# Turning the modulation's rows by 128x128 transposes, with the four groups added on VectorE

## The chip, the cores and the metric

The kernel runs on one core of one Trainium2 chip. The number that counts is the device time of one launch in microseconds (us), as the median of several runs. A profiled execution also leaves a trace, in which each instruction has an engine, a start and a duration.

## The reference, cut to what matters

```python
def first_block(x, c, ctx, c_ctx, w_mod, b_mod, ...):       # two layers, l = 0 and 1
    ...
    for l in range(DEPTH):
        mx = jnp.split((silu_c @ w_mod[l] + b_mod[l])[:, None, :], N_MOD, axis=-1)
        mc = jnp.split(silu_cc @ w_mod[l] + b_mod[l], N_MOD, axis=-1)
        # h = modulate(rms_norm(x), shift, scale): the mixer's input; a gate multiplies its output;
        # the same again for the MLP. mx is for the 256 tokens of x, mc for the 256 of ctx
```

The modulation of a layer is one row vector per condition (c for x, c_ctx for ctx) times a matrix of 1024 x 6144, plus a bias: 6 pieces of 1024, which are the shift, scale and gate of the mixer and of the MLP. The mixer has a Fourier branch, a latent attention branch (keys and values come from a narrow latent `ckv`, queries from `cq`) and a convolution branch, and ends with the product with `w_o`. After the first block comes a second one with another mixer (rwkv, s5 and gla branches), cross attention to a memory `mem`, and a feed-forward part. Everything is fp32.

## The kernel before

Activations lie with features on the 128 partitions and tokens in the free dimension. A large product is made from three products of split values: ScalarE casts a weight to a rounded high half (`wh<-raw`), VectorE subtracts to get the low half (`wl<-raw,wh`), and TensorE adds high x high, high x low and low x high in PSUM. Weights come in chunks of 512 KB (128 x 1024 fp32) through a pool `raw` of four buffers; one queue, SyncE's, issues these loads in the order in which the program asks for them, and a load waits there until its buffer is free.

The modulation of one layer is the generator `modulation(l)`, 24 steps of 256 columns, 48 steps in all. A step takes two loads of `w_mod`. It makes 8 products `md<-raw,cs`, whose stationary operand is the condition (32 columns, two of them used); each runs in one of four groups of 32 rows of the array, so that the group g = k % 4 leaves its partial row of condition i on partition 32g + i of a PSUM half bank. In the trace one such product has two records, so a step has 16. ScalarE copies the half bank to `mrow`. `end` then has to turn the row (columns must come to lie on partitions) and to add the four groups; VectorE adds the bias into `mod`. `end` of a step is called in the next step, so that TensorE has products ahead of it while ScalarE copies. Two half banks alternate.

These steps are fillers. In layer 0's norm, `mixer` calls for one step ahead of each of the eight norm pieces. In the mixer's branches, `weave` goes by a model of the engines' clocks (class `Core`): it takes the first chain whose operands are ready by that model, and prefers the filler where the model says that TensorE would otherwise be too idle. `need_mod` makes the steps that are still missing when a piece of the modulation is used: the first three pieces of layer 0 before `w_o`, the first of layer 1 late in layer 0's MLP. In layer 1's mixer the filler alternates between modulation steps and `memory()`, the keys and values of the second block's cross attention.

So the emitted order depends on the model's cost of every instruction. The model takes `product` for TensorE: an fp32 product costs four passes of the larger of its two widths plus 6 columns, a transpose two passes, and the number of counted columns goes into its notion of how busy TensorE was lately (2 x 2 x 2 for the selecting products of a step, up to 2 x 2 x 128 for two transposes). A scheduler then orders each engine's rows by a modelled time. All recorded instructions have line L243, a helper that passes calls on, so rows are told apart by tiles: `md`, `mrow` and `mod` are the modulation's, `mm` general products, `sc`, `prob` and `pt` attention, `ax` small sums and transposes, `cst_a` the constants (identity, ones and the selecting matrix `sel`).

Of the kernel before, what the change touches and what calls it, by code (L numbers as in the profile page):

```python
# [11 lines left out]
F32 = mybir.dt.float32  # L12
# [4 lines left out]
AX = mybir.AxisListType  # L17
PSUM = bass.MemoryType.PSUM

P = 128  # L20
# [471 lines left out]
class Prog:  # L492
# [241 lines left out]
    def modulation(self, l):  # L734

        nc = self.nc
        mod, ps2 = self.mods[l], self.mdp
        bm = self.v(f"b_mod{l}").rearrange("p (r h f) -> p r h f", r=3, h=2)  # L740
        mv = mod.rearrange("p i (r h f) -> p r h f i", r=3, h=2)

        def end(at, row, ps):
            for h in range(2):
                nc.tensor.matmul(ps[:, 2 * h:2 * h + 2], row[:, h * P:h * P + P], self.c("sel"), start=True, stop=True)
            r, f = at // KD, at % KD
            nc.vector.tensor_add(mv[:, r, :, f, :], ps[:, 0:4].rearrange("p (h i) -> p h i", i=2),
                                 bm[:, r, :, f].unsqueeze(2).to_broadcast([P, 2, 2]))
        last = raw = None

        def half(at, i):
            if l == 0 and self.first:
                return self.first.pop(0)
            return self.raw(self.a[f"w_mod{l}"][at, :, i * 1024:i * 1024 + 1024], 1024)
        for at in range(24):
            self.mark(f"mod{l}")
            raw = [raw or half(at, 0), half(at, 1)]
            ps = ps2[:, at % 2, :]

            for k in range(KD):  # L760
                g = k % 4
                nc.tensor.matmul(ps[32 * g:32 * g + 32, :], self.cs[:, k, :], raw[k // 4][:, k % 4 * T:k % 4 * T + T],
                                 start=k < 4, stop=k >= 4, tile_position=(0, 32 * g))
            row = self.c1.tile([P, T], F32, tag="mrow", bufs=2, name=self.nm("mrow"))
            nc.scalar.copy(row, ps)
            raw = half(at + 1, 0) if at < 23 else None
            if last is not None:
                end(*last)
            last = at, row, ps
            if at % KD == KD - 1:  # L770
                yield [row]
                self.mark(f"mod{l}")
                end(*last)
                last = None
                self.mod_done[l] = at // KD + 1
            yield [raw] if raw is not None else []
# [1736 lines left out]
```

## Time and profile before

| what | value |
|---|---|
| median of 3 runs | 1711.99 us (1711.25 to 1712.37) |
| the profiled execution | 1712.83 us, of which the trace's span is 1711.0 us |
| TensorE busy | 1621.9 us, 95% of the span |
| VectorE, ScalarE, GpSimd busy | 66%, 50%, 5% |
| mean granted TensorE clock | 0.972 of full speed |
| chain of work that ended last | TensorE 84%, VectorE 7%, ScalarE 4%, DMA 3%, issue 2% |
| modulation: the turning products | 192 records, 22.7 to 806.8 us |

The span runs from the first to the last recorded instruction; the execution's own time has 1.83 us more around it. Layer 0's mixer lies at about 25 to 270 us, its MLP up to 670 us, layer 1's mixer at 670 to 830 us, the second block from about 1060 us. A row of the busy table counts an engine's recorded work; a row of the chain says how much of the span is explained by that engine's work when the last instruction is followed back, releaser by releaser.

### The profile page before, as it was taken

The numbers are of one execution on the slowest core, as the hardware profiler recorded it, in microseconds if no ns is written. First come the engines' busy times: TensorE is split into PE (matmuls) and PEld (weight loads), VectorE is DVE, ScalarE is ACT, GpSimd is POOL, SyncE is SP. The second block draws the span as 40 slices with busy tenths as digits, with TensorE's granted clock in tenths as the row PEclk, the third lists the DMA queues.
The fourth block names the chain that finished last, engine by engine and source line by source line (L and its number), as shares of the span: only waits on it lengthen the run. The fifth ranks groups of instructions, "written<-read, shape, count | busy, mean of one in ns | idle before, by whom it ended". The sixth has DMA issues, their size and how long they took to land.

```text
span 1711.0 us, 32233 instructions
## 1 busy us (share of the span) xinstructions
PE 1621.9 (95%) x13240; PEld 1409.6 (82%) x13240; DVE 1123.1 (66%) x2051; ACT 853.2 (50%) x1479; POOL 77.1 (5%) x72
## 2 busy tenths in 40 slices
PE   5999999999999998899999999989989999999997
PEld 2676668888888886766999998878979899999997
DVE  4787536744444457667488866889446769788864
ACT  4436754542323234556565445732357647666643
POOL 0000001000000010000010001001200001010000
PEclk8999999999999999899999999999999999999999
DMA  7724562222322234445545554421113764345543
GB/s 265 238 81 155 189 237 97 84 92 96 99 99 98 87 117 148 172 166 182 180 162 187 184 181 162 147 100 64 40 59 126 253 204 168 124 157 189 177 163 105
DMA packets 69699, 249.61 MB, mean 146 GB/s; under 512 B 7728, under 2 KB 13104, under 8 KB 65712
## 3 DMA queue, kind: packets, MB, share of 16 engines
q1 hardware_dynamic: 69552, 247.55, 42.6%
q8 instruction: 104, 1.70, 0.4%
q14 instruction: 43, 0.35, 0.1%
HBM read 243.33 MB, written 4.19 MB: 145 GB/s over the span
## 4 chain that ended last, share of the span: by engine, by line
PE 84%; DVE 7%; ACT 4%; DMA 3%; issue 2%; SPq 0%; ACTq 0%; DVEq 0%
PE mm L243 65%; PE ax L243 10%; PE md L243 3%; PE sc L243 3%; PE fx L243 2%; DVE y L243 2%; DVE wl L243 2%; DMA raw<-w_mod 1%; ACT L243 1%; ACT wh L243 1%; DVE tmp L243 1%; DVE x L243 1%; DMA x<-xc 0%; ACT y L243 0%; DMA raw<-w_in 0%
## 5 line engine op out<-in xcount | busy, mean ns | idle before, releaser
L243 PE MATMUL mm<-hl,wh 128*128 128x256 f32 (+2 forms) x3856 | 861.3, 319 | 20.5 <-ACT wh L243 7.6
L243 PEld LDWEIGHTS mm<-hl,wh 128*128 128x128 f32 x3856 | 643.5, 193 | 79.8 <-ACT wh L243 9.8
L243 ACT CAST wh<-raw 128x1024 fp32r<-128x1024 f32 (+1 forms) x353 | 361.3, 1025 | 546.0 <-PE mm L243 426.5
L243 PE MATMUL mm<-hl,wl 128*128 128x256 f32 (+1 forms) x1928 | 611.8, 318 | 0.9 <-DVE wl L243 0.8
L243 DVE TENSOR_TENSOR wl<-raw,wh 128x1024 fp32r<-128x1024 f32 (+1 forms) x353 | 421.0, 1194 | 232.5 <-ACT wh L243 231.2
L243 PEld LDWEIGHTS mm<-hl,wl 128*128 128x128 f32 x1928 | 372.0, 193 | 27.2 <-DVE wl L243 3.3
L243 PE MATMUL mm<-y,wh 128*128 128x256 f32 x928 | 169.8, 285 | 7.5 <-DVE early L243 2.6
L243 PEld LDWEIGHTS mm<-y,wh 128*128 128x128 f32 x928 | 144.2, 191 | 9.7 <-DVE y L243 3.1
L243 DVE SCALAR_TENSOR_TENSOR x<-mm,mod,x 128x256 f32<-128x256 f32 x120 | 54.3, 480 | 118.0 <-PE mm L243 117.7
L243 PE MATMUL mm<-y,wl 128*128 128x256 f32 x464 | 131.2, 283 | 0.2 <-DVE wl L243 0.2
L243 POOL TENSOR_TENSOR sq<-sq,sq 128x256 f32<-128x256 f32 (+1 forms) x48 | 58.4, 1217 | 935.9 <-ACT sq L243 787.5
L243 PEld LDWEIGHTS mm<-y,wl 128*128 128x128 f32 x464 | 88.4, 191 | 0.5 <-DVE wl L243 0.4
L243 PE MATMUL mm<-hid,wh 128*128 128x512 f32 x256 | 80.4, 395 | 0.0
L243 PE MATMUL md<-raw,cs 128*32 128x256 f32 x768 | 63.5, 411 | 17.5 <-DMA raw<-w_mod 12.5
L243 DVE SCALAR_TENSOR_TENSOR acc<-u,vec,acc 128x512 f32<-128x512 f32 (+1 forms) x120 | 73.0, 613 | 1.8
L243 ACT ACT_TABLE_LOAD x47 | 60.3, 1283 | 7.9 <-DMA vec<-vec 3.6
L243 PEld LDWEIGHTS md<-raw,cs 128*32 128x32 f32 x768 | 20.1, 112 | 48.2 <-issue 12.2
L243 PEld LDWEIGHTS mm<-hid,wh 128*128 128x128 f32 x256 | 48.0, 187 | 11.7
L243 PE MATMUL mm<-hid,wl 128*128 128x512 f32 x128 | 50.6, 395 | 0.0
L243 DVE TENSOR_REDUCE mx<-sc 128x1 f32<-128x512 f32 (+1 forms) x56 | 31.9, 574 | 20.7 <-PE sc L243 20.3
L243 PE MATMUL sc<-k,hl 96*128 96x512 f32 (+1 forms) x144 | 42.7, 392 | 0.4 <-ACT prob L243 0.2
L243 ACT CAST hl<-tmp 128x256 fp32r<-128x256 f32 (+1 forms) x62 | 28.9, 471 | 27.0 <-DVE tmp L243 27.0
(393 smaller groups left out, 2010.4 us busy)
## 6 DMA issues: line engine op xcount, KB each, us to landing
raw<-w_mlp SPq DMA_DIRECT2D x128, 512.0 KB, 3.3
raw<-w_mod SPq DMA_DIRECT2D x96, 512.0 KB, 4.7
raw<-w_up SPq DMA_DIRECT2D x22, 1024.0 KB, 4.7
raw<-w_gate SPq DMA_DIRECT2D x24, 512.0 KB, 3.3
raw<-w_down SPq DMA_DIRECT2D x16, 704.0 KB, 4.1
raw<-w_in SPq DMA_DIRECT2D x20, 512.0 KB, 4.4
raw<-w_o SPq DMA_DIRECT2D x16, 512.0 KB, 3.9
raw<-w_rw SPq DMA_DIRECT2D x14, 512.0 KB, 3.8
```

Source lines behind the costliest of these rows:

```text
L243: return f(out, *args, **kw)
```

## The change

In `end`, two products of a 128x128 block of `mrow` (stationary) with the 128x2 selecting matrix, which turn the block and add the groups in one go, are replaced with two 128x128 transposes into the same PSUM half bank. The groups then stand side by side as columns 32g + i of each transposed block, and VectorE adds them with one `reduce_sum` over a strided view (4 results of 4 numbers per partition) into a new small tile `mdt` in SBUF with two buffers. The addition of the bias reads `mdt` in place of PSUM.

```diff
@@ -741,11 +741,13 @@
         mv = mod.rearrange("p i (r h f) -> p r h f i", r=3, h=2)
 
         def end(at, row, ps):
+
             for h in range(2):
-                nc.tensor.matmul(ps[:, 2 * h:2 * h + 2], row[:, h * P:h * P + P], self.c("sel"), start=True, stop=True)
+                nc.tensor.transpose(ps[:, h * P:h * P + P], row[:, h * P:h * P + P], self.c("ident"))
             r, f = at // KD, at % KD
-            nc.vector.tensor_add(mv[:, r, :, f, :], ps[:, 0:4].rearrange("p (h i) -> p h i", i=2),
-                                 bm[:, r, :, f].unsqueeze(2).to_broadcast([P, 2, 2]))
+            t = self.sm.tile([P, 2, 2], F32, tag="mdt", bufs=2, name=self.nm("mdt"))
+            nc.vector.reduce_sum(t, ps.rearrange("p (h g q) -> p h q g", h=2, g=4)[:, :, 0:2, :], axis=AX.X)
+            nc.vector.tensor_add(mv[:, r, :, f, :], t, bm[:, r, :, f].unsqueeze(2).to_broadcast([P, 2, 2]))
         last = raw = None
 
         def half(at, i):
```

The program has as many products as before on TensorE (10992 rows in all on that engine), but a transpose has one record in the place of two; VectorE has 48 more instructions (2101 in place of 2053), ScalarE 49 loads of its function tables in place of 47. The model's cost of `end` changes, and so does the order in which `weave` and the scheduler put the work. Steps of the modulation that are issued before layer 0's `w_o` number 40 and a half in place of 33 and a half; the rest follow in layer 1.

The first place is SyncE's queue in layer 0's input products, which issues the loads of weights (`raw_N` is a load's buffer, N only a running number). Before:

```order
L243 DMA raw_467<-w_in 128x1024
L243 DMA raw_473<-w_ukv 128x1024
L243 DMA raw_481<-w_mod 128x1024
L243 DMA raw_493<-w_mod 128x1024
L243 DMA raw_498<-w_in 128x1024
L243 DMA raw_543<-w_in 128x1024
L243 DMA raw_605<-w_in 128x1024
L243 DMA raw_645<-w_in 128x1024
```

And in the changed kernel, from the same load of `w_in` on:

```order
L243 DMA raw_483<-w_in 128x1024
L243 DMA raw_489<-w_ukv 128x1024
L243 DMA raw_497<-w_mod 128x1024
L243 DMA raw_509<-w_mod 128x1024
L243 DMA raw_516<-w_mod 128x1024
L243 DMA raw_528<-w_mod 128x1024
L243 DMA raw_547<-w_in 128x1024
L243 DMA raw_592<-w_mod 128x1024
L243 DMA raw_604<-w_mod 128x1024
L243 DMA raw_623<-w_mod 128x1024
L243 DMA raw_635<-w_mod 128x1024
L243 DMA raw_642<-w_in 128x1024
```

Eight loads of the modulation (four steps) stand ahead of the third chunk of `w_in` in place of two loads; before, the chunks of `w_in` followed one another from the fifth load on.

The second place is the end of layer 0's attention on TensorE: the attention's last products `mm<-pt,v`, steps of the modulation, and the first product with `w_o` (`mm<-hl,wh`). Before:

```order
L243 MATMUL mm_2070<-pt_2183,v_597 64x128
L243 MATMUL mm_2070<-pt_2209,v_597 64x128
L243 MATMUL md<-raw_2091,cs 32x256 x4
L243 MATMUL md<-raw_2140,cs 32x256 x4
L243 MATMUL md<-cst_a,mrow_2089 128x2 x2
L243 MATMUL md<-cst_a,mrow_2150 128x2 x2
L243 MATMUL md<-raw_2152,cs 32x256 x4
L243 MATMUL md<-raw_2192,cs 32x256 x4
L243 MATMUL md<-raw_2204,cs 32x256 x4
L243 MATMUL mm_2234<-hl_1020,wh_2224 128x512 x2
```

And in the changed kernel (the attention's last product stands four rows ahead of these, with `md<-raw` of 2216 and 2251 behind it):

```order
L243 MATMUL md<-raw_2263,cs 32x256 x4
L243 MATMUL md<-raw_2289,cs 32x256 x4
L243 MATMUL md<-cst_a,mrow_2261 128x128 x2
L243 MATMUL md<-raw_2301,cs 32x256 x4
L243 MATMUL md<-raw_2350,cs 32x256 x4
L243 MATMUL md<-cst_a,mrow_2299 128x128 x2
L243 MATMUL md<-raw_2362,cs 32x256 x4
L243 MATMUL md<-raw_2396,cs 32x256 x4
L243 MATMUL md<-cst_a,mrow_2360 128x128 x2
L243 MATMUL md<-cst_a,mrow_2406 128x128 x2
L243 MATMUL md<-raw_2408,cs 32x256 x4
L243 MATMUL mm_2431<-hl_1166,wh_2421 128x512 x2
```

The products of more steps stand between the attention and `w_o`: from the load named 2091 on before, from 2216 on now, that is, two and a half steps before and four and a half now. Each `md<-cst_a,mrow` row has a moving operand of 128 columns in place of 2.

The third place is TensorE in layer 1's input products, after the corrections `ax<-sh` that follow the first chunk of `w_in`; `mm<-wkh` are the values' products, whose operand `hl` comes from the latent by way of VectorE and ScalarE, and `ax<-sq` are sums of squares. Before:

```order
L243 MATMUL ax_5120<-sh_5117,wl_5018 128x2
L243 MATMUL md<-cst_a,mrow_5191 128x2 x2
L243 MATMUL ax_5206<-sq_5204,cst_a 128x512
L243 MATMUL md<-raw_5250,cs 32x256 x4
L243 MATMUL md<-raw_5306,cs 32x256 x4
L243 MATMUL md<-cst_a,mrow_5248 128x2 x2
L243 MATMUL md<-raw_5318,cs 32x256 x4
L243 MATMUL mm_5323<-wkh_5200,hl_5008 128x512
L243 MATMUL mm_5323<-wkl_5201,hl_5008 128x512
```

And in the changed kernel:

```order
L243 MATMUL ax_5317<-sh_5314,wh_5214 128x4
L243 MATMUL ax_5317<-sh_5314,wl_5215 128x2
L243 MATMUL mm_5472<-hl_5292,wl_5463 128x256
L243 MATMUL mm_5472<-hl_5292,wh_5462 128x256 x2
L243 MATMUL ax_5421<-sq_5419,cst_a 128x512
L243 MATMUL mm_5472<-hl_5292,wl_5463 128x256
L243 MATMUL mm_5498<-wkh_5415,hl_5205 128x512
L243 MATMUL mm_5498<-wkl_5416,hl_5205 128x512
```

The modulation's steps between the two are gone, and a second chunk of `w_in` (`mm<-hl,wl` and `mm<-hl,wh`, of which only some rows stand here) is ahead of the values' products.

## Rows read from the trace of the kernel before

**Rows 1.** The page, parts 1, 2 and 4: busy time, forty slices, chain by engine.

```profile
PE 1621.9 (95%) x13240; PEld 1409.6 (82%) x13240; DVE 1123.1 (66%) x2051; ACT 853.2 (50%) x1479; POOL 77.1 (5%) x72
...
PEclk8999999999999999899999999999999999999999
...
PE 84%; DVE 7%; ACT 4%; DMA 3%; issue 2%; SPq 0%; ACTq 0%; DVEq 0%
```

**Rows 2.** What touches tile md: count; minimum, median, maximum ns; first and last start.

```profile
L243 PE MATMUL md<-cst_a,mrow x192: 165/251/354, 22.7 to 806.8; 128*128 128x2 f32 x192
L243 DVE TENSOR_TENSOR mod<-md,vec x48: 145/165/169, 24.5 to 807.4; 128x4 f32<-128x4 f32 x48
```

**Rows 3.** The chain of waits in two stretches: start, duration, what, what released it.

```profile
41.26 0.48 PE md L243 x4
...
226.10 1.00 PE md L243 x16
...
228.68 0.88 PE ax L243 x8
229.55 0.34 PE md L243 x4
```

**Rows 4.** Timeline of TensorE at the same transposes: start, duration (records overlap), instruction.

```profile
228.51 1.04 PE L243 MATMUL ax<-cst_a,prob 128*128 128x128 f32 x8
```

**Rows 5.** VectorE's groups by form: two of its reductions.

```profile
L243 DVE TENSOR_REDUCE mx<-sc 128x1 f32<-128x512 f32 x32 | 22.1, 690 | 10.6 <-PE sc L243 10.4
L243 DVE TENSOR_REDUCE mx<-sc 128x1 f32<-128x256 f32 x24 | 9.8, 420 | 10.0 <-PE sc L243 9.9
```

**Rows 6.** Timeline of one turn of layer 0's norm: start, duration, engine, instruction.

```profile
44.34 0.61 PE L243 MATMUL md<-cst_a,mrow 128*128 128x2 f32 x4
45.05 0.17 DVE L243 TENSOR_TENSOR mod<-md,vec 128x4 f32<-128x4 f32 x1 [0.79 <-PE md L243]
...
47.53 0.61 PE L243 MATMUL md<-cst_a,mrow 128*128 128x2 f32 x4
```

**Rows 7.** Stretches: busy us (instructions) by engine, granted clock, DMA share, GB/s.

```profile
132.00:239.00 107.00, 104.82 (x848) 67.11 (x843) 60.50 (x148) 77.04 (x180) 0.00 (x0) 1.00 0.57 190
239.00:245.40 6.40, 3.42 (x33) 1.74 (x33) 0.71 (x4) 1.79 (x3) 0.00 (x0) 0.80 0.96 319
670.50:690.00 19.50, 12.54 (x80) 7.89 (x80) 9.17 (x18) 11.81 (x22) 4.57 (x6) 0.74 0.79 267
718.00:726.00 8.00, 4.14 (x36) 3.66 (x28) 4.30 (x10) 1.69 (x3) 0.00 (x0) 0.88 0.65 232
```

**Rows 8.** Timeline of layer 0's input products: a modulation step, the values' first product.

```profile
62.01 0.64 PE L243 MATMUL md<-raw,cs 128*32 128x256 f32 x8
...
70.59 0.50 PE L243 MATMUL mm<-wkh,hl 128*128 128x512 f32 x1
```

**Rows 9.** DMA issues from 20 to 80 us: count, size, median us to landing.

```profile
raw<-w_mod SPq DMA_DIRECT2D x18, 512.0 KB, 5.2
```

**Rows 10.** Timeline at the end of layer 0's attention: its last product, to w_o's first.

```profile
237.06 0.90 PE L243 MATMUL mm<-pt,v 128*64 128x128 f32 x8
...
239.02 16.76 SPq L243 DMA_DIRECT2D raw<-w_o  x8
...
245.35 1.22 PE L243 MATMUL mm<-hl,wh 128*128 128x512 f32 x2 [1.21 <-ACT wh L243]
```

**Rows 11.** Timeline of layer 1's input products: the latent's chain, and a load of w_uq.

```profile
679.38 1.23 DVE L243 TENSOR_TENSOR wl<-raw,wh 128x1024 fp32r<-128x1024 f32 x1 [0.45 <-ACT wh L243]
...
683.57 0.80 PE L243 MATMUL mm<-wkh,hl 128*128 128x512 f32 x1 [3.95 <-ACT hl L243]
```

**Rows 12.** The chain of waits in layer 1: two chunks of w_in, and the load of w_uq.

```profile
691.66 5.95 PE mm L243 x48
...
717.88 6.35 DMA raw<-w_uq
```

**Rows 13.** The chain of waits in the second block's mixer: a load of ScalarE's table.

```profile
1254.41 1.28 ACT L243
```

## The prediction

> **What bounds the kernel now.** I read the page first. TensorE is busy 95% of the span, the chain that ended last is TensorE for 84%, and the granted clock is near full in all slices but the first and one more [rows 1]. So on average a microsecond taken from TensorE is a microsecond won, and one added is lost; only where TensorE waits can work move for nothing. Next I looked at what touches the changed tile: 192 records of selecting products and 48 additions on VectorE, from 22.7 to 807 us [rows 2]; the second half of the program has none. Then the chain of waits, for what the turning costs where it lies on the chain, and last the stretches in which TensorE is not full: the wait ahead of layer 0's `w_o` (3.42 of 6.4 us busy) and two in layer 1 (12.54 of 19.5, and 4.14 of 8.0), against 104.82 of 107 us in layer 0's attention [rows 7]. These three places matter more than the average, since the order of the two programs differs there.
>
> **The turning itself.** On the chain, the four records of a step's selecting products take 0.48 and 0.34 us [rows 3]; I take 0.42. A transposing product of the same form (128x128 moving, fp32) is in the attention: eight take 0.88 us on the chain, 0.11 each [rows 3], and the timeline shows that these are 128x128 records, 1.04 us from the first one's start to the last one's end [rows 4], so that one lasts 1.04 - 7 x 0.11 = 0.27 and overlaps the next. Two make 0.22 if a transpose goes on having one record. So a step saves TensorE 0.2 us (0.42 - 0.22), with 0.12 and 0.26 as bounds from the two chain rows. A rule of the Trainium skill speaks against this: "TensorE: Matmul & The Clock Gate", Part 4, has a 128x128 transpose in one kernel's context at about 275 ns. By that page two would take 0.55 us, an estimate with it makes each step 0.13 us dearer and not 0.2 cheaper, and the whole change would come out near 1716.5. The trace agrees with the page on how long one record lasts, and differs on what eight cost, since they follow each other every 0.11 us.
>
> VectorE gets one reduction more in each step, four results from 16 numbers per partition. Its reductions take 690 ns for 512 numbers and 420 for 256 [rows 5]: 1.05 ns a number, so 420 - 240 x 1.05 = 168 ns for 16, which is also what the small addition takes [rows 2]. 48 of them are 8 us. In layer 0's attention VectorE is busy 60.5 of 107 us [rows 7], so there they hide beside TensorE; with that cover gone, the 39 steps behind the norm would pay 39 x 0.17 = 6.6 us.
>
> In layer 0's norm the two meet. A turn goes from 44.34 to 47.53 us, 3.2 us, and the addition waits 0.79 us for the turning and is waited for by the next norm piece [rows 6]. TensorE's share falls by 0.2, VectorE's rises by 0.17: nothing, for the first nine steps. Layer 0 has 33.5 steps ahead of `w_o`; without these nine and the 2.5 behind the attention, 22 are left: 22 x 0.2 = 4.4. In layer 1, 7.5 steps remain: 1.5. **The turning gives -5.9.**
>
> **Five steps moved into layer 0's full stretches.** By the order, seven steps (14 loads) leave layer 1 for layer 0: four among the chunks of `w_in`, one more up to the attention's end, and two behind it. A step's products cost 1.00 us on the chain [rows 3], with two transposes 1.22. Five make +6.1. The eight loads of the first four stand in SyncE's queue ahead of the third chunk of `w_in`. The products queued behind it on TensorE are those of `w_in`; in exchange the values' products, which begin at 70.59 us now [rows 8], stand ahead of that chunk. A load of `w_mod` lands 5.2 us after its issue in this stretch [rows 9]. Whether TensorE runs dry meanwhile no row of before shows: bounds 0 (covered by steps like that at 62.01 us [rows 8] and the values) and 5.2 (one whole landing); I take the middle, 2.5. **+8.6 (6.1 to 11.3).**
>
> **Two steps more behind the attention.** The attention's last product ends at 237.06 + 0.90 = 237.96, the first with `w_o` starts at 245.35: 7.4 us for 2.5 steps [rows 10]. There is nothing else to hide a step, so each passes ScalarE's copy, the turning, VectorE and the next products in a row; by 7.4 / 2.5 two more cost 5.9, by their products alone 2.4. The four loads, at the 319 GB/s of that stretch [rows 7] (0.524 MB / 319 GB/s = 1.64 us each), are 6.6. `w_o`'s loads are issued from 239.02 on behind those of the steps [rows 10], so they come later too. In this place the reduction isn't hidden. **+5.0 (2.4 to 6.6).**
>
> **Layer 1.** Of the seven steps, 3.5 leave its first stretch, and 3.5 later ones. The later ones lie beside full products: 1.00 + 0.42 = 1.42 each, -5.0 (bound -1.5, where they filled waits). In the first stretch TensorE waits for the values' operand until 683.57 for 3.95 us [rows 11]. That operand comes from `ckv` by VectorE and ScalarE; a `wl` subtraction of 1.23 us at 679.38 stands ahead of it on VectorE [rows 11], and in the changed order it does not, nor do the squares of `mem` stand ahead of its cast on ScalarE. I put the values' first product at 680, so 3.6 earlier. Besides, a second chunk of `w_in` now runs ahead of it, half of the 5.95 us for two [rows 12], 3.0 us that fall into the wait. Together -6.6; the bounds are 0 (a load is late in the operand's place) and -7.0, the stretch's whole idle time [rows 7]. Third, `w_uq`'s load is issued at 717.88 and lies on the chain for 6.35 us [rows 12], with 3.9 of 8 us idle [rows 7]; in the changed order it is issued ahead of the steps' loads. Late next are the queries' chain and the `w_in` chunks behind it. -4.0 (0 to -6.35). **Together -15.6.**
>
> **The second block's mixer** has two more loads of ScalarE's tables, 1.28 us each, and such loads lie on the chain today [rows 13]. That place has been put in another order, which the diff can't price. Half of 2.56: **+1.3 (-3 to +4,** the wider end for one table load more or two fewer on the chain).
>
> **The sum.** -5.9 + 8.6 + 5.0 - 15.6 + 1.3 = -6.6. The profiled execution took 1712.83 us, 0.84 above the median of the runs, its span 1711.0. 1712.83 - 6.6 - 0.84 = 1705.4; I say 1705.
>
> **The rivals.** A change of 0.2%, 3.4 us, is about what a measurement of this kernel can tell from none: faster is below 1708.6, slower above 1715.4.
>
> *The moves cancel.* The first stretch of layer 1 stays bound by the latent's chain: the products gone, TensorE waits as long for the values. For it: the wait there ends with ScalarE's cast of `hl`, not with a product, and DMA is busy 79% [rows 7, 11]. Against it: the subtraction ahead of the chain is gone in the order. It takes 6.6 from the gain: 1712.
>
> *Loads decide, and it gets slower.* In layer 1 both waits are for what comes late, not for products: the values' chain stays, and `w_uq`'s place is taken by another load that is as late. Of layer 1 only the 5.0 of the later steps is left, 10.6 less, and behind layer 0's attention each load costs its 1.64 us, +6.6 in place of +5.0. -6.6 + 10.6 + 1.6 = +5.6: 1717.6. It decides once the two waits give back less than 2.2 us (5.6 - 2.2 = 3.4). For it: DMA is busy 0.96 behind the attention and 0.65 to 0.79 in layer 1's waits [rows 7]. Against it: seven steps take 14 loads, 23 us at 1.64, out of layer 1's queue.
>
> *Transposes are dear.* Each record of the transposes takes its turn alone, its 0.27 us [rows 4], so two are 0.54 us and not 0.22: with 34.5 steps that are priced, 0.32 more each, +11.0: 1705.4 + 11.0 = 1716.4. Against it stand the eight in 0.88 us [rows 3]; for it, that here only two stand together, behind a wait for ScalarE's copy. The Trainium skill's page named above has that price.
>
> **How the numbers follow.** The forecast has 0.55: its terms come from rows, but the two largest, in layer 1, rest on how waits shrink. The cancelling case gets 0.22, the slower one 0.15, dear transposes 0.04; 0.04 is left for a gain of more than 15 us. The forecast's own range is 1698 to 1708.5: the bounds on the gain's side (tail 2.6, early load 2.5, `w_uq` 2.4, mixer 4.3) seldom come together, so I take 7 of their 11.8. The range for 8 in 10 reaches to the slower rival: 1697 to 1718. Faster: the forecast and the large gain without what spills over the bound, 0.56; same, the cancelling case and that spill, 0.24; slower 0.20.
>
> **What would show it.** The turning: 96 transposes with one record each, two in 0.22 us on the chain, and a reduction of 0.17 us; dear transposes would show 0.5. Layer 0's early place: the third chunk of `w_in` waits for its load, about 2.5 us of idle TensorE between 60 and 75 us. Its end: 12 to 13 us between the attention's last product and `w_o`'s first. Layer 1: the values' first product comes 3.6 us earlier against the layer's start, right behind two chunks of `w_in`, and no wait for `w_uq` remains. If the layer is not shorter by some 15 us, the prediction fails there. The second block: its length changed by more than 4 us would mean that its new order, not the modulation, decided.

## The result: slower, and the profile after

The changed kernel takes 1721.45 us (median of 7 runs, 1719.77 to 1723.54) against 1711.99 before (median of 7, 1703.29 to 1716.9): the ratio is 1.006, with a 95% interval of 1.0042 to 1.0078. I had forecast 1705, in a range of 1697 to 1718. The direction is wrong, and the time lies outside the range.

The page of the changed kernel (parts 1 and 4):

```profile
PE 1606.5 (93%) x13144; PEld 1393.1 (81%) x13144; DVE 1133.8 (66%) x2099; ACT 855.6 (50%) x1481; POOL 80.3 (5%) x72
...
PE 78%; DVE 11%; ACT 5%; DMA 3%; issue 2%; SPq 0%; POOL 0%; ACTq 0%; DVEq 0%; POOLq 0%
```

TensorE has 15 us less of work than in [rows 1], and still the span is 8.7 us longer (1719.7 against 1711.0): its idle time has grown from 89 to 113 us. In the chain VectorE's and ScalarE's work took over what TensorE lost. So the question is not what the transposes cost, but where TensorE waits.

The turning itself, by what touches `md` and `mdt` (count; minimum, median, maximum ns), and a turn of layer 0's norm on the timeline:

```profile
L243 PE MATMUL md<-cst_a,mrow x96: 270/273/476, 22.2 to 772.5; 128*128 128x128 f32 x96
...
L243 DVE TENSOR_REDUCE mdt<-md x48: 159/174/176, 23.7 to 774.2; 128x4 f32<-128x16 f32 x48
```

```profile
43.32 0.38 PE L243 MATMUL md<-cst_a,mrow 128*128 128x128 f32 x2
...
43.81 0.17 DVE L243 TENSOR_REDUCE mdt<-md 128x4 f32<-128x16 f32 x1 [0.54 <-PE md L243]
...
46.46 0.38 PE L243 MATMUL md<-cst_a,mrow 128*128 128x128 f32 x2
```

A transpose has one record, as forecast, and a reduction takes 0.17 us. A turn of the norm goes from 43.32 to 46.46, 3.14 us, against 3.19 in [rows 6]: what TensorE saves there, VectorE spends.

Now the places. One split of the program into five stages serves for all kernels here; its marks are the first and the last result of the first block that is added to `x`, the copy of layer 1's latent (`ckv<-early`) and the first load of `wq`. The row of `x` in the changed kernel, whose first and last start are two of the marks:

```profile
L243 DVE SCALAR_TENSOR_TENSOR x<-mm,mod,x x120: 471/483/486, 262.9 to 1064.5; 128x256 f32<-128x256 f32 x120
```

| stage (us) | before | changed | difference |
|---|---|---|---|
| layer 0's mixer, to the first result with `w_o` | 253.3 | 262.9 | +9.6 |
| rest of layer 0, to `ckv<-early` | 418.6 | 418.9 | +0.3 |
| layer 1, to the first block's last result | 392.0 | 382.7 | -9.3 |
| the second block's mixer, to the first load of `wq` | 366.9 | 378.5 | +11.6 |
| from there to the end | 280.2 | 276.7 | -3.5 |

The forecast for the first line, by its terms, was -4.4 + 8.6 + 5.0 = +9.2; for layer 1 -17.1, and for the second block +1.3. Stretches of layer 0 in the changed kernel (columns as in [rows 7]), TensorE's waits from 55 to 75 us (total, times, longest), and the end of the attention on the timeline:

```profile
60.00:70.00 10.00, 6.85 (x52) 3.24 (x52) 5.12 (x10) 5.13 (x8) 0.00 (x0) 0.79 0.67 240
129.60:239.00 109.40, 105.60 (x837) 67.28 (x837) 69.01 (x179) 78.90 (x185) 0.00 (x0) 1.00 0.57 191
239.00:253.80 14.80, 9.68 (x84) 3.10 (x82) 2.40 (x11) 3.11 (x6) 0.00 (x0) 0.76 0.95 327
```

```profile
PE md L243 <- DVE mdt L243: 1.6, 2, 1.3
PE md L243 <- ACT mrow L243: 1.5, 1, 1.5
```

```profile
238.24 0.93 PE L243 MATMUL mm<-pt,v 128*64 128x128 f32 x8
...
239.10 1.07 PE L243 MATMUL md<-raw,cs 128*32 128x256 f32 x16
...
241.44 0.64 PE L243 MATMUL md<-raw,cs 128*32 128x256 f32 x8 [0.34 <-DVE mdt L243]
...
244.88 0.64 PE L243 MATMUL md<-raw,cs 128*32 128x256 f32 x8 [0.69 <-DMA raw<-w_mod]
...
246.74 7.33 SPq L243 DMA_DIRECT2D raw<-w_o  x4
...
248.20 1.94 PE L243 MATMUL md<-raw,cs 128*32 128x256 f32 x16 [0.34 <-DVE mdt L243]
...
252.76 1.04 ACT L243 CAST wh<-raw 128x1024 fp32r<-128x1024 f32 x1 [2.19 <-DMA raw<-w_o]
...
253.86 1.22 PE L243 MATMUL mm<-hl,wh 128*128 128x512 f32 x2 [0.18 <-ACT wh L243]
```

From 60 to 70 us TensorE stands still for 3.15 us, where it was busy for all 10 before. I had put a standstill here at 2.5, but for the third chunk of `w_in`, and that isn't what TensorE waits for: that chunk is issued at 69.02, and no wait for a load is listed. It waits for the steps' own copy (`mrow`) and sum (`mdt`). They stand in line on ScalarE and VectorE behind the cast and the subtraction of an earlier chunk, issued at 60.69. In the attention it is nearly as full as before (105.60 of 109.4 us). Behind it, the last product ends at 239.17, and the first one with `w_o` begins at 253.86: 14.7 us, against 7.4 in [rows 10], with TensorE at half its clock for much of it (0.76 on average). `w_o`'s first load is issued at 246.74, and ScalarE waits 2.19 us to cast it; but TensorE is at work on steps meanwhile, and waits only 0.18 us for that cast. What fills the stretch is the steps. One whose loads are there takes 2.34 us (239.10 to 241.44); the next two take 3.44 and 3.32, with waits for loads of `w_mod` in them (0.69 is one).

Layer 1 from the latent's copy to the attention's last product, before and in the changed kernel, and the stretch ahead of the values in the latter:

```profile
671.90:817.10 145.20, 128.43 (x957) 97.79 (x956) 101.53 (x222) 86.11 (x171) 4.57 (x6) 0.93 0.52 180
...
681.80:819.80 138.00, 114.85 (x821) 92.15 (x819) 104.78 (x224) 83.30 (x164) 6.30 (x6) 0.93 0.40 132
684.70:693.90 9.20, 1.53 (x8) 0.78 (x7) 8.43 (x16) 5.47 (x7) 0.00 (x0) 0.81 0.86 274
```

TensorE's longest waits there in the changed kernel, two of those of before, and two instructions of VectorE in the changed kernel's stretch ahead of the values:

```profile
PE mm L243 <- ACT hl L243: 7.7, 1, 7.7
PE ax L243 <- ACT prob L243: 3.4, 4, 1.8
PE sc L243 <- ACT prob L243: 2.6, 1, 2.6
```

```profile
PE mm L243 <- ACT wh L243: 3.8, 1, 3.8
...
PE ax L243 <- ACT prob L243: 0.4, 2, 0.2
```

```profile
686.70 1.22 DVE L243 TENSOR_TENSOR wl<-raw,wh 128x1024 fp32r<-128x1024 f32 x1
...
688.40 1.23 DVE L243 TENSOR_TENSOR wl<-raw,wh 128x1024 fp32r<-128x1024 f32 x1
```

Here the moved work is gone: TensorE is busy 114.85 us. The same stage of before had 128.43 busy in 145.2. But its idle time has grown from 16.8 to 23.2 us. The wait for the values' operand, which was 3.95 us in [rows 11] and was to shrink, is 7.7 now: from 684.7 to 693.9 VectorE is busy 8.43 of 9.2 us, TensorE 1.53. Two subtractions `wl` of the weights stand there ahead of the latent's chain, and the values start 12.0 us after the latent's copy, 11.7 before. The wait of 3.8 us for the cast of `w_uq` is gone, as forecast, but waits for the softmax (`prob`) have grown from 0.4 to 6.0 us.

The second block's mixer as a stretch, before and in the changed kernel, and TensorE's waits behind ScalarE there, changed kernel first and then before:

```profile
1063.90:1430.80 366.90, 342.61 (x4792) 318.05 (x4793) 257.27 (x471) 190.86 (x306) 16.91 (x16) 0.96 0.37 126
```

```profile
1064.50:1443.00 378.50, 342.82 (x4795) 318.34 (x4796) 258.66 (x471) 192.25 (x306) 17.28 (x15) 0.96 0.35 122
```

```profile
PE mm L243 <- ACT gla_go L243: 10.4, 2, 6.1
...
PE mm L243 <- ACT y L243: 4.6, 2, 4.4
```

```profile
PE mm L243 <- ACT gla_go L243: 2.0, 1, 2.0
```

Nothing of the modulation runs there. TensorE has the same work at the same granted clock, so nearly all of the 11.6 us is idle time. Its products wait for PSUM banks that ScalarE has yet to empty (`gla_go`, the gla branch's gate) and for operands that it casts (`y`); ScalarE has 49 loads of tables at 1.28 us in the whole program, in place of 47. The Trainium skill, "ScalarE: Activation LUTs", section "What ACT_TABLE_LOAD costs", has 1283 ns for a load and a drain of about 1380 ns with it; the trace agrees on the load, and in its chain the next work on ScalarE starts 0.01 us behind one, so no drain shows.

### The profile page after: what moved, and what is told of

Read it like the earlier page. It is cut to its first block, busy times and chain, and to the rows that moved or that the text cites. A ratio compares the mean times of both kernels' runs of the same rounds, so it can differ in the third digit from the quotient of the medians.

```text
span 1719.7 us, 32095 instructions
## 1 busy us (share of the span) xinstructions
PE 1606.5 (93%) x13144; PEld 1393.1 (81%) x13144; DVE 1133.8 (66%) x2099; ACT 855.6 (50%) x1481; POOL 80.3 (5%) x72
## 4 chain that ended last, share of the span: by engine, by line
PE 78%; DVE 11%; ACT 5%; DMA 3%; issue 2%; SPq 0%; POOL 0%; ACTq 0%; DVEq 0%; POOLq 0%
PE mm L243 62%; PE ax L243 9%; PE md L243 3%; DVE y L243 3%; PE sc L243 3%; DVE wl L243 2%; ACT L243 1%; ACT wh L243 1%; DVE tmp L243 1%; PE fx L243 1%; DMA raw<-w_mod 1%; DVE hl L243 1%; DVE rw_m L243 1%; DVE acc L243 1%; DMA raw<-w_in 1%
## 5 line engine op out<-in xcount | busy, mean ns | idle before, releaser
L243 PE MATMUL mm<-hl,wh 128*128 128x256 f32 (+2 forms) x3856 | 859.5, 319 | 27.0 <-ACT gla_go L243 10.4
L243 PEld LDWEIGHTS mm<-hl,wh 128*128 128x128 f32 x3856 | 642.4, 193 | 85.9 <-ACT gla_go L243 10.9
L243 PE MATMUL md<-raw,cs 128*32 128x256 f32 x768 | 60.0, 414 | 19.0 <-ACT warm L243 7.9
L243 ACT ACT_TABLE_LOAD x49 | 62.9, 1283 | 4.9 <-DMA vec<-vec 3.6
```

The costliest lines, as they stand in the source:

```text
L243: return f(out, *args, **kw)
```

## The experiments

Two theories. **A:** the turning by transposes is cheaper, and the loss comes from the order, which the model of costs changes along with `end`: in layer 0, in layer 1 and, by accident, in the second block. **B:** the turning itself is the loss, by transposes that cost 0.27 us or by VectorE's reductions. All stages are in the table behind the last experiment. Each ratio is to the runs of before up to then (medians 1712.3, 1712.67 and 1710.16 us in the three rounds).

**New turning, old plan.** The model that `weave` goes by is told of the old instructions (`note` is its entry); the new ones are issued past it. The scheduler behind it sees what is really issued, so a plan fixes what `weave` emits, and rows can still change places:

```diff
+                nc.note("pe", "matmul", ps[:, 2 * h:2 * h + 2], (row[:, h * P:h * P + P], self.c("sel")), {})
-                nc.tensor.transpose(ps[:, h * P:h * P + P], row[:, h * P:h * P + P], self.c("ident"))
+                nc.nc.tensor.transpose(ps[:, h * P:h * P + P], row[:, h * P:h * P + P], self.c("ident"))
...
+            nc.note("dve", "tensor_add", to, (ps[:, 0:4].rearrange("p (h i) -> p h i", i=2), bias), {})
```

> The transposes and the reduction are issued, but the model of the order is told of the selecting products and of the one addition, so that the steps stand where they stood before (33.5 ahead of layer 0's w_o). Theory A (the order made the loss, the turning itself saves about 0.2 us a step): w_o's first load is issued 2 to 5 us earlier than before (before at about 239 us of the span), layer 1 ends no later. Theory B (the turning itself is dear, 0.2 to 0.35 us more a step, because transposes take 0.27 us each and VectorE's reduction lies on the path): the same place comes 5 to 10 us later than before. The second block's order also comes out differently here, so the total says less than the stages.

Measured: 1693.62 us, ratio 0.9897 (0.9864 to 0.993). `w_o`'s first result comes 11.1 us earlier and its first load 12.2, more than the 2 to 5 that theory A gave for the load. Its timeline at the end of layer 0's attention and its row of `x`:

```profile
233.25 0.73 PE L243 MATMUL mm<-hl,wh 128*128 128x512 f32 x2 [0.96 <-ACT wh L243]
...
238.01 0.65 PE L243 MATMUL mm<-pt,v 128*64 128x128 f32 x6
```

```profile
L243 DVE SCALAR_TENSOR_TENSOR x<-mm,mod,x x120: 471/483/486, 242.2 to 1045.0; 128x256 f32<-128x256 f32 x120
```

The scheduler puts products with `w_o` (`mm<-hl,wh`, from 233.25) among the attention's last products (`mm<-pt,v`, still at 238.01), so the stretch behind the attention is gone. It isn't shown how much of the 11.1 us comes of that.

**Old turning, new plan.** The mirror image: the model is told of the transposes and the reduction, the selecting products and the one addition are issued.

```diff
+                nc.note("pe", "transpose", ps[:, h * P:h * P + P], (row[:, h * P:h * P + P], self.c("ident")), {})
-                nc.tensor.transpose(ps[:, h * P:h * P + P], row[:, h * P:h * P + P], self.c("ident"))
+                nc.nc.tensor.matmul(ps[:, 2 * h:2 * h + 2], row[:, h * P:h * P + P], self.c("sel"), start=True, stop=True)
```

> The selecting products and the one addition are issued, but the model is told of the transposes and the reduction, so that the steps stand as in the changed kernel (40.5 ahead of w_o). Theory A: w_o's first load is issued 7 us later than before, as in the changed kernel, or up to 5 us more, since the dearer turning is done 40 times there; layer 1 gives back about 9 us. Theory B: it is issued no later than before, since the dear turning is gone.

Measured: 1721.16 us, ratio 1.0059 (1.0037 to 1.0081). `w_o`'s first result comes at 270.7, 17.4 us later than before and 7.8 later than in the changed kernel. `w_o`'s first load, which theory A put 7 to 12 us later than before, is issued 17.8 us later. Theory B falls: without the transposes layer 0 is longer, not shorter. Yet the total is that of the changed kernel: the second block, whose rows the scheduler orders otherwise here, takes 371.9 us and not 378.5.

**Only the second block's order.** 2.2 us are added to the model's clocks at the start of the second block, in the kernel before; 1.7 us in the changed kernel.

```diff
     def block2(self):
+        for q in self.nc.clock:
+            self.nc.clock[q] += 2.2
```

> The kernel before, with 2.2 us added to the clocks of the model of the order at the start of the second block and nothing else: every instruction up to there stands as before, the second block's mixer comes out in another order, in which the preparation of the gla branch stands late, as in the changed kernel. Theory A (12 us of the loss are the second block's order, which hangs on the model's clock and not on transposes): 5 to 15 us slower than before, all of it between 1200 and 1360 us. Theory B (the modulation is the loss): within 0.2% of before.

> The changed kernel, with 1.7 us added to the model's clocks at the start of the second block and nothing else: the modulation and both layers stand as in the changed kernel, the gla branch's preparation stands about 40 products earlier and 44 loads of tables are issued in place of 49. Theory A: 8 to 15 us faster than the changed kernel, so 1706 to 1714, within 0.3% of before. Theory B: as slow as the changed kernel, 1720 to 1723.

Measured: 1730.92 us, ratio 1.0119 (1.0093 to 1.0145), so a shift of the model's clock alone costs twice what the whole change did, and more than the 5 to 15 us that theory A gave; and 1716.15 us, ratio 1.0013 (0.9997 to 1.0029), which is not to be told from before. That is 5.3 us below the changed kernel, less than the 8 to 15 of theory A, and clear of theory B. The stages put it in the second block's mixer (the first one's profiled run took 1724.93, 6 us under its median): 383.3 us against 366.9, and 372.4 against 378.5. TensorE's waits in the first of the two:

```profile
PE mm L243 <- ACT y L243: 9.6, 2, 6.3
PE mm L243 <- ACT gla_go L243: 6.2, 3, 4.3
```

**Is it the evacuations behind loads of tables?** In the changed kernel the gate is copied, without its function; the model is told of the function, so that TensorE's order stays as it was.

```diff
-            nc.scalar.activation(go[m], ps[:, :T], AF.Silu)
+            nc.note("act", "activation", go[m], (ps[:, :T], AF.Silu), {})
+            nc.nc.scalar.copy(go[m], ps[:, :T])
```

> The changed kernel, but the gla branch's output gate is copied out of PSUM in place of going through the silu function (that function is left out; the model is told of it as before, so that TensorE's and SyncE's orders are those of the changed kernel). A copy needs no table, so 44 loads of tables are left of 49. Theory A (in the second block TensorE waits for PSUM to be emptied by ScalarE, which stands in line behind loads of tables): the waits for the gate's evacuations go from 10.4 us to under 3, and the second block's mixer is 6 to 11 us shorter. Theory B (the gla branch's late preparation makes the loss by itself): the mixer is shorter by 2 us at most, since the preparation stands where it stood.

```profile
PE mm L243 <- ACT gla_go L2096: 6.2, 2, 4.6
...
PE mm L243 <- ACT y L243: 4.6, 2, 4.4
```

The wait for the gate goes from 10.4 to 6.2 us and the mixer from 378.5 to 374.6. That is between the two theories: the gate's function, and with it five loads of tables (44 are left), is 4 of the 11.6 us. The rest of this wait isn't for the gate's own table, and the casts behind `y` wait as long as before. Total 1716.24, ratio 1.003 (1.0014 to 1.0046).

**The price of each new part, by multiplying it.** In the changed kernel, three more pairs of transposes in each step, and in another three more reductions, none of them told to the model:

```diff
+            for h in (0, 1) * 3:
+                nc.nc.tensor.transpose(ps[:, h * P:h * P + P], row[:, h * P:h * P + P], self.c("ident"))
```

```diff
+            for _ in range(3):
+                nc.nc.vector.reduce_sum(t, ps.rearrange("p (h g q) -> p h q g", h=2, g=4)[:, :, 0:2, :], axis=AX.X)
```

> The changed kernel with three more pairs of the same transposes in every step (288 more, into the same half bank; the model of the order is not told of them, the scheduler behind it is). Layer 0 up to the attention's last product holds some 36 steps, so 216 more transposes. Theory A (a transpose costs TensorE 0.11 us): that place comes 24 us later than in the changed kernel. Theory B (0.27 us each): 58 us later. From two records of a few hundred ns in the trace the pace of eight in a row should be seen directly, 0.9 us or 2.2 us.

> The changed kernel with three more of the same reductions in every step (144 more, 0.17 us each, 24 us of VectorE's time; the model is not told). Theory A (VectorE's part is hidden where TensorE is full, and lies on the path only in layer 0's norm and behind its attention): 0.5 us in each of the nine steps of the norm and the five behind the attention, so layer 0 is 4 to 8 us longer, layer 1 as long. Theory B (the reduction is on the path everywhere): 20 to 24 us.

The chain of waits with the multiplied transposes (the step's own two, then the six more):

```profile
235.19 0.22 PE md L243 x2
235.41 0.66 PE md L748 x6
```

Six in 0.66 us, 0.11 each, and the pair ahead of them in 0.22. The 275 ns of the Trainium skill's "TensorE: Matmul & The Clock Gate", Part 4, is what one record lasts here, not what one costs. Layer 0's mixer is 19.0 us longer for some 240 more transposes, and the kernel takes 1735.52 (ratio 1.0139, 1.011 to 1.0167). So the rival of dear transposes is out.

The reductions turned out worse than both theories said (4 to 8 us, or 20 to 24): layer 0's mixer is 28.3 us longer, 291.2, the kernel 1742.11 (ratio 1.0182, 1.0156 to 1.0209). Its attention, to be held against the second row of the stretches above:

```profile
133.40:264.90 131.50, 117.24 (x837) 71.02 (x837) 78.52 (x241) 79.29 (x185) 0.00 (x0) 0.91 0.47 159
```

As many records (837) take 117.24 us in place of 105.60, at a granted clock of 0.91 in place of 1.00, and TensorE is idle 14.3 us in place of 3.8. VectorE is busy only 60% of it. So a busy share of 57 to 63% was no cover for three more in each step: among TensorE's longest waits in this stretch are those for the softmax (3.1 us, `prob`) and for the reductions (2.5 us, `mdt`), which stand in line on VectorE with the attention's maxima. Layer 1 is 2.5 us longer. This is no price of the change's one reduction: with that one alone, the clock in the attention stayed at 1.00.

In both kernels of this pair the second block comes out in another order again, and its mixer takes 368.5 and 367.7 us in place of 378.5, though `weave` follows the changed kernel's plan.

**Seven steps of layer 1 left out**, in the kernel with the new turning and the old plan (their loads stay):

```diff
+            out = l == 1 and 10 <= at <= 16
...
+                if out:
+                    nc.note("pe", "matmul", ops[0], ops[1:], {})
+                else:
+                    nc.tensor.matmul(*ops, start=k < 4, stop=k >= 4, tile_position=(0, 32 * g))
```

> The kernel with the new turning in the old plan (turn_new_plan_old), with seven steps of layer 1 left out, but for their loads (products, copy, transposes and sums; their pieces of the modulation stay zero). The model is told of them as before. Theory A (steps of layer 1 fill waits, so moving them out gives little back): layer 1's mixer from the latent's corrections to the attention's last product is 0 to 3 us shorter than in turn_new_plan_old (139.6 us there). Theory B (my forecast's prices, 1.2 to 1.4 us a step and the waits that they prolong): 8 to 15 us shorter.

```profile
PE md L243 <- DMA raw<-w_mod: 10.4, 3, 7.6
PE mm L243 <- ACT hl L243: 7.1, 1, 7.1
```

Neither theory holds. By the measure named, the latent's copy to the attention's last product, the kernel takes 150.1 us against 139.6; and to the first block's last result 395.8, against 385.6 to 390.4 with the seven steps. TensorE now waits 10.4 us for loads of `w_mod` and 7.1 for the values' operand. The scheduler put other rows in other places, so this is no clean subtraction; in this order at least, taking work out of the stage gave nothing. Total 1710.58, ratio 0.9992 (0.9975 to 1.001).

**The loads behind layer 0's attention.** In the changed kernel the steps 36 to 40 load nothing; their products read `x`, so that part of the modulation is not computed.

```diff
+                if l == 1 and 12 <= at <= 16:
+                    ops = *ops[:2], self.x[k][:, :T]
```

> The changed kernel, in which the steps 36 to 40 (those behind layer 0's attention) load nothing: their products read values of x in place of w_mod, so nine loads of 512 KB are gone and that part of the modulation is wrong; the model is told as before. Theory A (loads make the stretch behind the attention long, w_o's loads above all, which stand in the queue behind those of the steps): from the attention's last product to the first result with w_o it takes 15 us or less, as before the change (15.4), against 23.7 in the changed kernel. Theory B (the row of copy, transposes, reduction and products decides, about 3 us a step): 20 us or more remain.

```profile
238.75 0.73 PE L243 MATMUL mm<-hl,wh 128*128 128x512 f32 x2 [0.50 <-ACT wh L243]
...
256.86 1.07 PE L773 MATMUL md<-x,cs 128*32 128x256 f32 x16 [0.96 <-DVE mdt L243]
...
259.20 1.07 PE L773 MATMUL md<-x,cs 128*32 128x256 f32 x16 [0.34 <-DVE mdt L243]
```

By the measure that I had named theory A holds (14.9 us), but the measure was a bad one: products with `w_o` now start at 238.75 among the attention's, and the first result still comes at 259.9, only 3.0 us earlier, since steps without a load still stand ahead of the last of them. 3.0 us is no more than identical orders differ by (below the table), so it prices nothing. The rows do: without loads a step takes 2.34 us here (256.86 to 259.20), as it did in the changed kernel where its loads were there, against 3.3 to 3.4 with the wait for them. So the steps' own row of copy, transposes, reduction and products is the larger part, and loads some 1 us a step. Total 1717.26, ratio 1.0015 (0.9986 to 1.0043).

**The latent's chain in layer 1.** In the changed kernel GpSimd makes the low halves of two chunks of `w_in` in layer 1. They were meant to be the two whose subtractions stand ahead of the latent's chain on VectorE.

```diff
+            if src.name == "w_in1" and self.nin in (3, 4):
+                nc.note("dve", "tensor_sub", l[:, :e - s], (w[:, s:e], h[:, :e - s].bitcast(F32)), {})
+                nc.nc.gpsimd.tensor_sub(l[:, :e - s], w[:, s:e], h[:, :e - s].bitcast(F32))
```

> The changed kernel, with the low halves of two chunks of w_in in layer 1 (the two that stand ahead of the latent's norm on VectorE) made by GpSimd; the model is told of VectorE. Theory A (layer 1's values wait for the latent's chain on VectorE, in which two subtractions of 1.23 us stand): the values' first product comes 1.5 to 3 us earlier after the latent's copy than the 12.0 us of the changed kernel. Theory B (it waits for the loads of w_in or for TensorE itself): 12 us as before, or later.

```profile
PE mm L243 <- ACT hl L243: 6.5, 1, 6.5
```

```profile
685.06 1.23 DVE L243 TENSOR_TENSOR wl<-raw,wh 128x1024 fp32r<-128x1024 f32 x1
...
686.76 1.23 DVE L243 TENSOR_TENSOR wl<-raw,wh 128x1024 fp32r<-128x1024 f32 x1
```

The edit missed its place: it moved the two subtractions ahead of these (at 678.02 and 681.97 in the changed kernel), and the two in the stretch itself still stand on VectorE. The wait falls from 7.7 to 6.5 us, the values start 11.6 us after the copy in place of 12.0, and the layer goes from 382.7 to 382.1. So whether those two subtractions hold the values up stays untested. The total is 1721.0, ratio 1.0045 (1.0019 to 1.0071).

**The better version, with the second block moved.** The kernel with the new turning and the old plan, with 0.8 and with 2.2 us added to the model's clocks as above.

> The kernel with the new turning in the old plan (turn_new_plan_old, 1693.6 us), with 0.8 us added to the model's clocks at the start of the second block. The gla branch's preparation stands 42 products earlier, and its four gate evacuations stand behind one another with one load of a table in place of two. Theory A (evacuations behind loads of tables make the second block's length): TensorE's wait for the gate falls from 5.9 us to under 3, and the kernel takes 1688 to 1693. Theory B (the orders differ by chance in many places, so that one place tells nothing): anything from 1690 to 1705.

> The same with 2.2 us added: the second block's order is now nearly that of the changed kernel (its ScalarE has the same 49 loads of tables, its TensorE all but 372 of 5341 products in the same place), while both layers stand as in turn_new_plan_old. Theory A (the second block's order costs by itself, whatever the modulation does): from the first load of w_rw to that of wq it takes 378 to 383 us, as in the changed kernel (380.6), against 369.2 in turn_new_plan_old, and the kernel takes 1701 to 1706. Theory B (the changed kernel's second block is long for another reason, such as its modulation): 369 to 372 us, and 1693 to 1696.

Measured: 1697.66 (ratio 0.9908, 0.9881 to 0.9936) and 1707.02 (0.997, 0.9942 to 0.9999). TensorE's waits in the second of them:

```profile
PE mm L243 <- ACT gla_go L243: 10.4, 2, 6.1
PE mm L243 <- ACT y L243: 5.9, 2, 3.1
```

With the changed kernel's order of the second block come the changed kernel's waits (10.4 us for the gate) and nearly its length (376.9 against 378.5), though the layers are those of the fast version. The first one shortened the gate's wait, and others came for it: its mixer takes 368.0, no less than 367.1. So theory A holds for the second, whose order costs by itself, and fails for the first, for which it gave 1688 to 1693.

The stages of all kernels (us, one profiled execution each):

| kernel | layer 0's mixer | rest of layer 0 | layer 1 | second mixer | rest |
|---|---|---|---|---|---|
| before | 253.3 | 418.6 | 392.0 | 366.9 | 280.2 |
| before_block2_moved | 253.8 | 418.5 | 389.0 | 383.3 | 278.6 |
| turn_old_plan_new | 270.7 | 418.5 | 382.3 | 371.9 | 277.0 |
| changed | 262.9 | 418.9 | 382.7 | 378.5 | 276.7 |
| after_block2_moved | 262.1 | 419.1 | 381.5 | 372.4 | 277.8 |
| gate_copied | 263.1 | 417.8 | 381.6 | 374.6 | 277.1 |
| latent_first | 262.4 | 418.2 | 382.1 | 377.5 | 275.2 |
| tail_without_loads | 259.9 | 416.0 | 382.8 | 378.8 | 278.7 |
| transposes_x4 | 281.9 | 418.4 | 388.9 | 368.5 | 276.6 |
| reductions_x4 | 291.2 | 418.5 | 385.2 | 367.7 | 276.9 |
| turn_new_plan_old | 242.2 | 417.2 | 385.6 | 367.1 | 276.8 |
| turn_new_block2_a | 244.3 | 417.2 | 390.4 | 368.0 | 277.1 |
| turn_new_block2_b | 245.6 | 417.2 | 388.5 | 376.9 | 277.1 |
| layer1_seven_out | 243.1 | 417.7 | 395.8 | 376.2 | 276.0 |

The three kernels turn_new_plan_old, turn_new_block2_a and turn_new_block2_b have the same order in both layers, and yet differ by 3.4 us in the first column and by 4.8 in the third. Differences of that size between two profiles say nothing here.

## Why the prediction was wrong

Two axes tell it, turning and plan, from the table (a plan, as said, fixes the rows only in part). **The turning**, at the same plan: layer 0's mixer goes from 253.3 and 253.8 (selecting products) to 242.2, 244.3 and 245.6 (transposes), about -9.5, and in the new plan from 270.7 to 262.9, -7.8. In layer 1 it is -2 in the old plan and nothing in the new one. I had -4.4 for layer 0 and -1.5 for layer 1. The sign and the price of a transpose (0.11 us) were right, the size in layer 0 was short: -7.8 over 40 steps is the 0.2 us a step of the forecast, but on all steps, not on the 22 that I had counted. In the old plan the scheduler also lets `w_o`'s products in among the attention's, which is likely the rest. In totals the turning gives 18.7 us in the old plan and nothing in the new one (1721.16 against 1721.45), where the second block's order takes back what layer 0 gains. **The plan**, at the same turning: layer 0's mixer +17.4 with selecting products and +18.9 with transposes (262.9 less the mean 244.0), layer 1 some -8 and -5.5.

Step by step. Layer 0's +9.6 is near the forecast's +9.2 by luck, since its terms miss both ways. *To the attention's last product* the forecast had -4.4 + 8.6 = +4.2, and it ends 1.2 us later (239.17 against 237.96). With selecting products in the new plan it ends at 248.8, so the five early steps cost some 10.9 and the turning gives some 9.6 of it back: both terms were too small. The standstill of 3.15 us had the forecast size and another cause. *The two steps behind the attention* (+5.0, at most 6.6) were too small: 14.7 us against 7.4 is +7.3. Two steps in a row take 2 x 2.34 = 4.7, the wait for their loads some 2 more by the rows above, and the granted clock is 0.50 from 248.2 to 253.8. I had taken the middle of the bounds where the upper one was the like case. The last 1.0 us comes behind `w_o`'s first product, and I had nothing for it.

*Layer 1* (-15.6, with the turning -17.1) is one of the two steps that failed. It gave back 9.3, 7.2 of it up to the attention's last product. The three terms rested on waits that would shrink once the steps were gone. The wait for the values' operand, for which I had taken -3.6, grew from 3.95 to 7.7 us: the chain of VectorE and ScalarE behind it ends no earlier than before (12.0 us after the copy against 11.7), and the steps had been filling the time. I had read from the order that no subtraction stands ahead of that chain any more; two do, of later chunks (686.70 and 688.40). The wait for `w_uq` did go. TensorE's work in this stage fell by 13.6 us (128.43 to 114.85) and its idle time rose by 6.4. This is the rival of the moves that cancel, whose place and mechanism I had named and given 0.22. The later steps gave back less too: TensorE waits in their place for the softmax (3.4 and 2.6 us for `prob`).

*The second block's mixer* (+1.3, bounds -3 to +4) is the other step that failed, and the larger: +11.6, from a change that does not touch it. I had priced two loads of tables; what came instead is idle time of TensorE, with the same work, 8.4 us of it in the wait for the gate alone. The experiments show that the order by itself does this (before_block2_moved +16.4 us in this stage, after_block2_moved -6.1, turn_new_block2_b +9.8), and that a shift of the model's clock at the block's start is enough for it, without any transpose. Why the other parts of the order are long, beyond the gate's 4 us, stays open. So does what makes the -3.5 at the end: the other kernels have 275.2 to 278.6 there, which points to the profiled execution of before as long, rather than the changed one as short.

The rival that ended on the other side gave 1717.6 by loads; the time is near it, but its mechanism is not what decided: loads account for some 1 us a step behind the attention, and layer 1 did give something back. The sum, from the stages: +9.6 + 0.3 - 9.3 + 11.6 - 3.5 = +8.7, the difference of the spans. Without the second block's +11.6 the change would have come out about where it was, and with the old plan it is 1% faster than before.

## What to carry to other kernels

Where a model of costs writes the order, a change of one instruction is two changes; tell the model the old costs and the new instructions, and the other way round, and measure both before judging the instruction. Here the instruction, told to the model at the old costs, is worth some 12 to 19 us (1697.66 against 1710.16, and 1693.62 against 1712.3), and the order that came with the new costs takes all of it and more. Work moved out of a stage whose waits end with another engine's chain gave back less than its own length, and a place that the change does not touch deserves a range as wide as its reordering has been seen to move it.

## What the runs showed of the chip

A fp32 transpose of 128x128 lasts 0.27 us and is followed by the next after 0.11, even in a lone pair. VectorE at 60% busy was no cover for 0.5 us more in each step: with the reductions multiplied TensorE was idle 14.3 us of layer 0's attention in place of 3.8, its granted clock there fell from 1.00 to 0.91 on average, and 837 records were busy 11.6 us longer. And the same instructions in the same order differed by up to 4.8 us in one layer (385.6 to 390.4) from one profile to the next.
